# A list scheduler's assumed operand delay for TensorE, its price of a tile change and its priorities are replaced: encoder layer with RWKV-7 and differential attention, one core

## The chip, the cores and the metric

The kernel runs on one core of a Trainium2 chip. The time is device microseconds (us) of one execution. Engines are named as in the profile: PE (TensorE matmuls), PEld (TensorE weight loads), DVE (VectorE), ACT (ScalarE), POOL (GpSimd), SP (the queue that issues every DMA).

## The reference, cut to what matters

One encoder layer over two sequences (256 and 512 tokens, together T = 768, width 1024), in float32:

```
xn   = rmsnorm(x, norm_mix);  proj = xn @ w_in                  # 67 tiles of 128 columns
r, k, v, lw, la, lg = split(centred_shift(proj[:RWKV_COLS], mu)) # 27 of the tiles
y_a  = rwkv7_mixer(...)       # two scans (forward, backward) of 64x64 states, 16 heads
y_b  = diff_attention(...)    # 8 heads, partial rotary, two softmaxes each
merged = sigmoid(gate_a) * (y_a @ proj_a) + sigmoid(gate_b) * (y_b @ proj_b)
h    = x + merged @ w_out
out  = rmsnorm(h + square(relu(rmsnorm(h) @ w_mlp_in)) @ w_mlp_out, norm_final)
```

## The kernel before, in words

**The work.** Large products are split into three matmuls of a rounded type (fp32r: high by high, low by high, high by low), with 384 or 512 columns; the small ones of the scan and of attention are plain fp32. Operands of the large ones lie in region `x` (activations and weights), so the trace shows them as `bank<-x`. A weight comes by DMA in pieces of 128x256, one engine (ACT or DVE) rounds it to the high half, DVE subtracts to get the low half (`split`, called from `proj`), and only then TensorE can use it. PSUM has eight banks.

The scan is done in chunks of 64 tokens. There are 8 pairs of heads, and for each 4 jobs (two directions by two halves of the tokens), 32 in all. A job runs: `front` (decays, keys), group `g1` (matmuls 128x192), `solve` (a triangular inverse), `g2`, `duo` and `chain`. `solve` writes a matrix to DRAM, reads it back in another layout onto 96 partitions, runs 31 dependent steps on POOL (tile `f<-f`), writes the result to DRAM (`td`, four DMAs) and reads it back (four DMAs into `T_` and four into `tb`). Then DVE transposes 32x32 blocks (line 677), TensorE does a first half (six matmuls of 64x32 outputs), ACT or DVE copies the result, and TensorE does the second half (twelve matmuls 32x32). `duo` does groups of 128x128 matmuls, and `chain` carries the state from chunk to chunk: two matmuls with 64 columns, a copy from PSUM, two matmuls, and so on; each link needs the copy of the one before.

The projections that the scan doesn't need ("extra", 40 tiles of 48 matmuls) may stand anywhere and fill the time between. After the scans come attention (mixed with the last extras and `proja`), `projb`, `wout`, and the MLP.

**What sets the order.** `layer` first records some 18,500 operations with their dependencies in a `Plan`; `Plan.schedule` then simulates the five engines and emits, engine by engine, in the order that it chose. Every instruction is in-order on its engine, so this order is the kernel. At each step the scheduler takes the engine that is free first and, of the operations that are ready there, the one with the smallest key. The key is the place in the program (pair and job) plus `SHIFT` of the stage's name; `BIAS` decides, for work that more than one engine can do, which takes it; `LATE` says how many of the late pieces (`rest`) are recorded ahead of each attention head. When something is ready is worked out so, with `end` the simulated end of the operation it needs:

```
for s in o.next:
    s.wait -= 1
    for f in s.forms:
        s.ready[f] = max(s.ready[f], clk[e] if e == f == "pe" else end + AFTER[f])
```

and the choice on TensorE adds a price where the array's tile (128x128, 64x128, 128x64, 32x32) changes:

```
switch = lambda o: SWITCH * (e == "pe" and o.forms[e][2][0] != clock.tile)
for k, n, r, o in sorted((o.key + TURN * turns(o, e) + switch(o), o.n, r, o) for r, o in avail[e] if r <= t + 1e-3):
```

The simulated times and keys exist only while the program is built; on the chip nothing waits for them.

## Time and profile before

| | |
|---|---|
| median of 3 runs | 1998.9 us (1997.29 to 1999.33) |
| the profiled execution | 1998.35 us |
| its span, first to last instruction | 1996.5 us |
| PE busy | 1938.1 us (97%) |
| DVE busy | 1259.4 us (63%) |
| ACT busy | 871.9 us (44%) |
| POOL busy | 828.5 us (41%) |
| mean granted TensorE clock | 0.989 |

The page's share of busy time says which engine to look at; where that one stands still, and at which clock it runs, is read by stretches of the span. Stretches (us from the start): 0 to 28 norm of the input, 28 to 1050 projections and scans, 1050 to 1300 attention, 1300 to 1450 `projb` and `wout`, from 1450 the MLP. A matmul's end is modelled in the trace, so a busy PE is not a PE at its peak; an idle one surely waited.

### The profile page before, as it was taken

To read this page: it belongs to the slowest core of one execution; us is meant where nothing else is said; L and a number is where in the kernel's file an instruction comes from. 1 tells how busy PE (TensorE), PEld (TensorE's weight loads), DVE (VectorE), ACT (ScalarE), POOL (GpSimd) and SP (SyncE) were. 2 spreads that over 40 slices of the span, in tenths; PEclk is the share of its full clock that TensorE was granted. 3 is DMA by queue.
4 is the path that set the end of the run, shared out by engine and by line. 5 is a ranking of instruction groups with operands and counts; after the bars stand their busy time and mean duration, and the time that the engine had idled before them with its cause. 6 is when DMAs were issued, how large, how long until landed. Compare 5 with 4: busy or idle time off the path is not lost.

```text
span 1996.5 us, 36368 instructions
## 1 busy us (share of the span) xinstructions
PE 1938.1 (97%) x12698; PEld 1729.2 (87%) x12698; DVE 1259.4 (63%) x2750; ACT 871.9 (44%) x2178; POOL 828.5 (41%) x2177
## 2 busy tenths in 40 slices
PE   6999989999999999999999999999999999999998
PEld 6988879888888989889888776899899899989997
DVE  6977575666767677577534878574475555555545
ACT  5635465555656556565444778442221111111113
POOL 3278778786877878888770011011100000000000
PEclk9999999999999999999999999999999999999999
DMA  4133332222323232232343342254121111111111
GB/s 152 55 110 97 86 84 75 76 70 73 92 66 98 76 79 80 81 88 59 93 121 107 107 143 76 81 174 139 45 85 64 63 64 64 64 64 64 64 48 64
DMA packets 209787, 169.09 MB, mean 85 GB/s; under 512 B 106817, under 2 KB 176194, under 8 KB 209602
## 3 DMA queue, kind: packets, MB, share of 16 engines
q1 hardware_dynamic: 209602, 166.76, 28.1%
q8 instruction: 100, 1.64, 0.4%
q14 instruction: 85, 0.70, 0.1%
HBM read 137.97 MB, written 28.70 MB: 83 GB/s over the span
## 4 chain that ended last, share of the span: by engine, by line
PE 80%; DVE 11%; DMA 3%; ACT 2%; SPq 2%; issue 2%; POOL 0%; DVEq 0%; ACTq 0%; POOLq 0%
PE bank L693 78%; DVE g L622 3%; PE bank L698 2%; DVE x L622 2%; SPq L618 2%; DVE f L627 1%; DVE f L632 1%; DMA g<-dram 1%; DVE f L622 1%; DMA g<-in_w_in_dram 1%; DVE g L632 0%; DVE f L1012 0%; ACT f L669 0%; ACT x L638 0%; DVE g L677 0%
## 5 line engine op out<-in xcount | busy, mean ns | idle before, releaser
L693 PE MATMUL bank<-x 128*128 128x384 f32 (+1 forms) x5296 | 1146.9, 362 | 13.0 <-DVE x L622 4.6
L693 PEld LDWEIGHTS bank<-x 128*128 128x128 f32 x5296 | 929.6, 189 | 113.3 <-issue 18.9
L622 POOL TENSOR_TENSOR f<-f 96x60 f32<-96x60 f32 (+25 forms) x2081 | 758.9, 367 | 241.1 <-ACT f L638 41.5
L622 DVE TENSOR_TENSOR x<-g,x 128x256 fp32r<-128x256 f32 (+3 forms) x490 | 252.6, 522 | 159.7 <-ACT x L638 149.8
L693 PE MATMUL bank<-f,g 128*128 128x384 f32 x1920 | 338.2, 337 | 1.6 <-ACT f L669 1.6
L693 PEld LDWEIGHTS bank<-f,g 128*128 128x128 f32 x1920 | 336.1, 187 | 2.6 <-ACT f L669 1.9
L638 ACT ACTIVATE x<-g 128x256 fp32r<-128x256 f32 (+2 forms) x336 | 149.8, 453 | 351.6 <-PE bank L693 282.0
L622 DVE TENSOR_TENSOR g<-bank,g 128x128 f32<-128x128 f32 (+4 forms) x380 | 178.0, 479 | 179.2 <-PE bank L693 143.2
L638 ACT ACTIVATE g<-bank 64x128 f32<-64x128 f32 (+6 forms) x659 | 203.8, 324 | 189.3 <-PE bank L693 152.8
L622 POOL TENSOR_TENSOR g<-g 128x512 f32<-128x512 f32 (+1 forms) x9 | 15.4, 1711 | 592.3 <-DVE g L622 580.8
L693 PE MATMUL bank<-g,f 128*128 128x64 f32 (+3 forms) x1568 | 245.1, 293 | 4.5 <-DVE g L622 2.1
L693 PEld LDWEIGHTS bank<-g,f 128*128 128x128 f32 x1568 | 218.1, 191 | 27.0 <-DVE f L622 3.8
L622 DVE TENSOR_TENSOR g<-g 128x384 f32<-128x384 f32 (+6 forms) x234 | 116.7, 502 | 86.2 <-ACT g L669 73.8
L669 ACT ACTIVATE g<-bank 128x384 f32<-128x384 f32 x96 | 46.3, 491 | 246.5 <-PE bank L693 246.1
L638 ACT ACTIVATE f<-bank 128x192 f32<-128x192 f32 (+6 forms) x268 | 95.4, 387 | 109.9 <-PE bank L693 95.8
L693 PEld LDWEIGHTS bank<-g,g 64*128 64x128 f32 (+1 forms) x1728 | 119.7, 193 | 22.5 <-ACT g L638 10.7
L693 PE MATMUL bank<-g,g 64*128 64x128 f32 (+1 forms) x1728 | 136.5, 287 | 1.4 <-ACT g L638 1.4
L639 DVE CAST x<-g 128x384 fp32r<-128x384 f32 (+2 forms) x156 | 56.6, 364 | 54.7 <-PE bank L693 40.4
L698 PE MATMUL bank<-h,g 128*128 128x128 f32 x392 | 67.9, 294 | 19.0 <-DVE g L647 14.3
L693 PE MATMUL bank<-f 128*128 128x256 f32 (+2 forms) x352 | 86.0, 483 | 0.0
L693 PEld LDWEIGHTS bank<-g 32*32 32x32 f32 (+2 forms) x1378 | 54.8, 130 | 34.8 <-DVE g L677 14.4
L693 PE MATMUL bank<-g 32*32 32x32 f32 (+3 forms) x1378 | 73.9, 225 | 10.5 <-DVE g L677 9.0
(80 smaller groups left out, 1356.8 us busy)
## 6 DMA issues: line engine op xcount, KB each, us to landing
g<-in_w_in_dram SPq DMA_DIRECT2D x268, 128.0 KB
g<-in_w_dram SPq DMA_DIRECT2D x128, 256.0 KB
f<-dram SPq DMA_DIRECT2D x112, 192.0 KB
dram<-g SPq DMA_DIRECT2D x80, 192.0 KB
g<-in_x_dram SPq DMA_DIRECT2D x12, 512.0 KB
g<-dram SPq DMA_DIRECT2D x32, 192.0 KB
f<-dram SPq DMA_DIRECT2D x32, 144.0 KB
g<-in_pb_dram SPq DMA_DIRECT2D x16, 256.0 KB
```

Of the source, the lines that this page charges most:

```text
L618: pl.op([("sp", us, lambda: nc.sync.dma_start(out=chip(out), in_=chip(in_)), None)], [in_], [out], n / 250e3, tail)
L622: form = lambda x: (NAME[x], cost(x, (a, b), out), lambda: x.tensor_tensor(out=chip(out), in0=chip(a), in1=chip(b), op=op), None)
L627: emit = lambda: V.tensor_scalar(out=chip(out), in0=chip(a), scalar1=chip(s1), scalar2=chip(s2), op0=o0, op1=o1)
L632: emit = lambda: V.scalar_tensor_tensor(out=chip(out), in0=chip(a), scalar=chip(s), in1=chip(b), op0=o0, op1=o1)
L638: S: ("act", cost(S, (a,), out), lambda: S.activation(out=chip(out), in_=chip(a), func=AF.Copy, scale=1.0), None),
L639: V: ("dve", cost(V, (a,), out), lambda: V.tensor_copy(out=chip(out), in_=chip(a)), None),
L669: S.activation(out=chip(out), in_=chip(a), func=fn, scale=chip(scale), **k)
L693: emit = lambda: TE.matmul(chip(out), lhsT=chip(lhsT), rhs=chip(rhs), start=start, stop=stop)
L698: pl.op([("pe", 0.112, lambda: TE.transpose(chip(out), chip(a), chip(ident)), ((P, P), True, 0))], [a, ident], [out], tail=0.165)
```

## The change

Five tables of numbers are changed, and no line of the computation:

```
-AFTER = dict(pe=0.053, act=0.034, dve=0.033, pool=0.077, sp=0.026)
+AFTER = dict(pe=0.453, act=0.034, dve=0.033, pool=0.077, sp=0.026)
-SWITCH = 1.24
+SWITCH = 2.44
-LATE = (4, 4, 4, 3, 3, 4, 4, 2)
+LATE = (4, 4, 4, 3, 5, 4, 4, 2)
-SHIFT = {'proja': 3.64, 'rotate': -7.5, 'vs': -19.94, 'attn': -2.04, 'solve': -1.61, 'attend': -3.24, 'kkn': -4.92, 'proj': 4.76, 'g1': 1.9, 'g2': -1.95, 'chain': 1.9, 'norm': -6.88, 'x': -4.47, 'const': -7.99, 'lora': -10.39, 'front': 0.93, 'duo': -2.19, 'finish': -0.48, 'extra': 0.92, 'head': 3.89, 'projb': -6.52, 'wout': 18.65, 'mlp': -1.8}
-BIAS = {'x': {'dve': -0.25, 'act': 0.68, 'pool': -0.82}, 'a': {'dve': 2.31, 'pool': 5.49, 'act': -0.17}, 'b': {'dve': 0.49, 'pool': 4.32, 'act': -0.19}, 'c': {'act': -0.05, 'pool': 1.31, 'dve': 0.09}}
+SHIFT = {'proja': 3.68, 'rotate': -5.61, 'vs': -20.91, 'attn': -7.05, 'solve': -2.9, 'attend': -2.08, 'kkn': -4.32, 'proj': 4.7, 'g1': 1.71, 'g2': -1.95, 'chain': 1.9, 'norm': -6.7, 'x': -4.47, 'const': -8.17, 'lora': -9.73, 'front': 0.93, 'duo': -2.05, 'finish': -2.34, 'extra': 0.37, 'head': 2.79, 'projb': -6.57, 'wout': 17.42, 'mlp': -0.98}
+BIAS = {'x': {'dve': -0.67, 'act': 0.68, 'pool': -1}, 'a': {'dve': 2.31, 'pool': 5.25, 'act': 0.35}, 'b': {'dve': 0.49, 'pool': 4.03, 'act': -0.19}, 'c': {'act': 0.57, 'pool': 1.4, 'dve': 0.09}}
```

The scheduler now takes what another engine makes for TensorE as usable 0.4 us later than before, a tile change as twice as dear, and the stages' priorities are new numbers. The same operations are emitted: 10,177 matmuls and 1,373 DMAs in both; 45 fewer on ACT (2,010 to 1,965 activations), 31 more casts (237 to 268) and 15 more copies (91 to 106) on DVE, 19 more two-input operations on POOL (2,125 to 2,144). The order differs almost everywhere. Three places:

TensorE, the two halves of the 19th of the 32 solves; `64x32` is the first half, `32x32` the second, `bank<-x` are large matmuls of projections that don't depend on it. Before:

```order
L693 MATMUL bank_80<-x_88 128x384 x3
L693 MATMUL bank_76<-g_105 64x32 x6
L693 MATMUL bank_77<-x_88 128x384 x2
L693 MATMUL bank_79<-g_91 32x32 x2
L693 MATMUL bank_81<-g_91 32x32 x2
L693 MATMUL bank_79<-g_91 32x32 x2
L693 MATMUL bank_81<-g_91 32x32 x2
```

Now:

```order
L693 MATMUL bank_78<-x_88 128x384 x3
L693 MATMUL bank_80<-g_105 64x32 x6
L693 MATMUL bank_82<-x_88 128x384 x3
L693 MATMUL bank_78<-x_88 128x384
L693 MATMUL bank_75<-g_91 32x32 x2
L693 MATMUL bank_76<-g_91 32x32 x2
L693 MATMUL bank_75<-g_91 32x32 x2
L693 MATMUL bank_76<-g_91 32x32 x2
```

Four independent matmuls stand between the halves where there were two. Over the 32 solves the median goes from 2 to 4.

TensorE, links of the chain in the same job; `128x64` are the links (`g` the state's matrices, `f` what the copy has just written). Before:

```order
L693 MATMUL bank_78<-g_91,f_97 128x64 x2
L693 MATMUL bank_76<-x_88 128x384 x3
L693 MATMUL bank_78<-g_91,f_97 128x64 x2
L693 MATMUL bank_79<-x_88 128x384 x3
L693 MATMUL bank_78<-g_91,f_97 128x64 x2
```

Now:

```order
L693 MATMUL bank_78<-g_91,f_97 128x64 x2
L693 MATMUL bank_75<-x_88 128x384 x2
L693 MATMUL bank_80<-x_88 128x384 x3
L693 MATMUL bank_75<-x_88 128x384
L693 MATMUL bank_78<-g_91,f_97 128x64 x2
L693 MATMUL bank_75<-x_88 128x384 x2
```

Six stand between links where there were three; over all links that follow each other in one bank the commonest number goes from 3 (75 of 156) to 6 (82 of 161).

The SP queue, around the 18th solve; `dram<-f` 192x1x32 are its four result writes, `32x6x32` and `32x3x32` from the same `dram` its read-back, `128x768` the store of a finished pair, `dram<-g` 32x6x32 the input of a later solve. Before:

```order
L618 DMA dram_1934<-f_97 192x1x32
L618 DMA f_97<-in_glora_dram 128x128
L618 DMA g_91<-in_w_in_dram 128x256
L618 DMA dram_7156<-g_91 128x768
L618 DMA dram_1934<-f_97 192x1x32 x3
L618 DMA dram_882<-g_91 32x6x32
L618 DMA g_91<-dram_1934 32x6x32
L618 DMA g_91<-dram_1934 32x3x32
```

Now:

```order
L618 DMA dram_1875<-f_97 192x1x32 x4
L618 DMA f_97<-in_glora_dram 128x128
L618 DMA dram_7161<-g_91 128x768
L618 DMA g_91<-dram_1875 32x6x32
L618 DMA g_91<-dram_1875 32x3x32
```

The four writes stand together, and the later solve's input is behind the read-back. Over the 32 solves, DMAs of other work between a solve's first write and its last read-back go from 161 to 113, and those of them that are stores from 88 to 43.

## Rows read from the trace of the kernel before

**Rows 1.** The page's busy time of each engine.

```profile
PE 1938.1 (97%) x12698; PEld 1729.2 (87%) x12698; DVE 1259.4 (63%) x2750; ACT 871.9 (44%) x2178; POOL 828.5 (41%) x2177
```

**Rows 2.** Busy time by stretch, instructions in brackets; then TensorE clock, DMA share, GB/s.

```profile
core 0: us, PE busy (x) PEld busy (x) DVE busy (x) ACT busy (x) POOL busy (x), PEclk, DMA share, GB/s
0.00:28.00 28.00, 11.01 (x50) 9.38 (x51) 20.56 (x30) 19.84 (x43) 15.11 (x23) 0.88 0.56 189
28.00:100.00 72.00, 71.18 (x418) 69.11 (x417) 59.42 (x132) 41.21 (x93) 18.41 (x33) 1.00 0.23 70
100.00:600.00 500.00, 478.14 (x3740) 429.99 (x3738) 332.33 (x806) 265.13 (x704) 385.77 (x1069) 0.98 0.30 83
600.00:950.00 350.00, 347.12 (x2813) 314.31 (x2806) 246.75 (x564) 207.56 (x544) 285.32 (x782) 1.00 0.29 80
950.00:1050.00 100.00, 95.24 (x788) 86.51 (x788) 46.00 (x107) 48.22 (x134) 76.28 (x235) 0.97 0.39 110
1050.00:1450.00 400.00, 397.89 (x2173) 329.06 (x2171) 260.08 (x581) 210.57 (x499) 43.59 (x34) 1.00 0.35 108
1450.00:1985.00 535.00, 534.34 (x2720) 488.55 (x2721) 288.37 (x522) 74.56 (x151) 4.00 (x3) 1.00 0.19 62
1985.00:1997.00 12.00, 3.18 (x15) 2.29 (x13) 5.88 (x13) 4.82 (x13) 0.01 (x1) 0.74 0.42 160
```

**Rows 3.** Waits of PE's matmuls: for whom, us in total, times, longest.

```profile
PE bank L698 <- DVE g L647: 14.3, 4, 9.7
PE bank L693 <- DVE g L677: 9.0, 7, 2.9
PE bank L693 <- DVE x L622: 4.6, 10, 0.7
PE bank L693 <- ACT x L638: 4.3, 4, 3.1
PE bank L698 <- ACT g L648: 3.0, 1, 3.0
PE bank L693 <- DVE g L622: 2.4, 3, 1.9
PE bank L693 <- ACT f L669: 2.1, 2, 1.6
PE bank L693 <- DVE x L639: 1.5, 3, 1.1
PE bank L693 <- ACT g L638: 1.4, 2, 0.8
...
PE bank L693 <- DVE g L632: 0.2, 1, 0.2
```

**Rows 4.** Timeline, 443 to 449 us: start, length, engine, line, operation.

```profile
442.94 2.84 SPq L618 DMA_DIRECT2D g<-dram  x6
447.23 0.77 DVE L677 STREAM_TRANSPOSE g<-g 32x192 f32<-32x192 f32 x2 [3.93 <-DMA g<-dram]
448.06 0.85 PE L693 MATMUL bank<-g 128*64 128x32 f32 x12 [2.89 <-DVE g L677]
```

**Rows 5.** Timeline, 1012 to 1022 us.

```profile
1014.88 3.88 SPq L618 DMA_DIRECT2D g<-dram  x6
1017.88 0.42 ACT L638 ACTIVATE x<-g 128x256 fp32r<-128x256 f32 x1 [4.67 <-DMA g<-in_w_in_dram]
1018.35 3.18 PE L693 MATMUL bank<-x 128*128 128x384 f32 x9 [3.11 <-ACT x L638]
```

**Rows 6.** Timeline of PE, 560 to 575 us.

```profile
559.79 0.52 PE L693 MATMUL bank<-x 128*128 128x384 f32 x2
560.16 0.52 PE L698 MATMUL bank<-h,g 128*128 128x128 f32 x3
560.43 8.94 PE L693 MATMUL bank<-x 128*128 128x384 f32 x50
```

**Rows 7.** POOL's instructions on tile f: ns least, median, most; first and last start.

```profile
L622 POOL TENSOR_TENSOR f<-f x2081: 197/312/1587, 36.3 to 1049.4; 96x60 f32<-96x60 f32 x20, 128x256 f32<-128x256 f32 x11, 96x28 f32<-96x28 f32 x10, 96x66 f32<-96x66 f32 x10
```

**Rows 8.** Casts on DVE, by form: busy us, mean ns, idle before.

```profile
L639 DVE CAST x<-g 128x384 fp32r<-128x384 f32 x69 | 24.9, 361 | 2.4
```

## The prediction

> **What bounds the kernel now.** I read the page's busy times first, then busy time by stretch, the waits of PE, and the timeline around the two longest waits in the middle. TensorE is busy 97% of the span and the next engine 63% [rows 1], so the time is PE's work plus what PE loses. The stretches show where it loses [rows 2]. In the first 28 us it idles 17.0 us while the input is loaded and normalised, and in the last 12 us it idles 8.8: neither contains scan work, and I book nothing there. In between it is idle 0.8 + 21.9 + 2.9 + 4.8 + 2.1 + 0.7 = 33.2 us (length of each stretch less PE's busy time), nearly all of it from 100 to 600 and 950 to 1050 us. In these two the granted clock is also lower: 0.98 of 500 us and 0.97 of 100 us, so 10 + 3 = 13 us of full-speed time lost to the lower of the clock's two levels, 1.2 GHz. From 1050 us on the clock is at 2.4 GHz (1.00) and idle time is 2.8 us until the tail. So a different order of the same matmuls can win at most about 33 + 13 = 46 us, and only where scans and projections are mixed.
>
> The waits say what PE stood for [rows 3]. Transposes and copies for the start (line 698, 14.3 and 3.0 us) are in the first stretch. The others are three kinds. (a) The transposed read-back of a solve (line 677): 9.0 us in 7 waits, up to 2.9. (b) Rounded weights (tile `x`): 4.6 + 4.3 + 1.5 = 10.4 us in 17 waits, up to 3.1. (c) Results of ACT and DVE that go back to PE, the other groups: 2.4 + 2.1 + 1.4 and seven smaller ones of 1.3 down to 0.2, together 10.9 us, each under 2 us. Kinds (a) and (b) are DMAs that came late. At 448 us six read-back DMAs were issued in 2.84 us, DVE waited 3.93 us for them, and PE 2.89 us for DVE [rows 4]; at 1018 us a weight's DMA stood with six read-backs of 3.88 us in the SP queue, ACT waited 4.67 us for it and PE 3.11 us [rows 5].
>
> **The change part by part.** No operation is added or removed on PE or SP. What is moved, counted from the order: two more large matmuls between the halves of a solve, three more between the links of a chain. One such matmul takes 8.94 / 50 = 0.179 us [rows 6], so the cover grows by 0.36 and 0.54 us. Between a solve's first write and its last read-back stand 113 other DMAs instead of 161, and 43 stores instead of 88; a store waits in the queue for the engine that makes its data, and holds the read-back behind it.
>
> *(c), results of ACT and DVE.* At 10.9 us in some 20 waits their mean is about 0.55 us, as much as the added cover. Bounds: 0 (the longer ones are of late engines) and 10.9. I take -6, a little over half, since a few are 1.6 to 1.9 us long [rows 3] and would keep over 1 us.
>
> *(a), read-back.* Bounds 0 and 9.0. PE's use of the transposed blocks planned 0.4 us later takes 7 x 0.4 = 2.8 us by itself; the shorter queue takes more: a DMA of this queue costs 2.84 / 6 = 0.47 us of issue [rows 4], and (161 - 113) / 32 = 1.5 fewer stand in each solve's way, 0.7 us. Together about 1.1 us of a mean wait of 1.3 us. The longest keep a part, so I take -5.
>
> *(b), weights.* Bounds 0 and 10.4. Only the last hop is moved 0.4 us earlier; the 3.1 us wait would keep most of its length if the same DMAs met, 16 waits share the other 7.3 us and are no longer than about 1.1. I take -4.
>
> *The clock.* Bounds 0 and 13. The lower level follows the waits in these stretches (0.98 and 0.97 there, 1.00 in the stretch between with 2.9 us of idle in 350) [rows 2]. With 15 of some 30 us of waits gone I take the same half: -6.
>
> *The tile price.* Over PE's whole order the tile changes go from 378 to 372, the changes between fp32r and fp32 matmuls from 1,011 to 1,059. Around such a piece two large matmuls start within 0.37 us (0.185 each against 0.179), and the three small ones within 0.27 [rows 6]: no price above 0.1 us is visible. 48 x 0 to 0.1 gives 0 to +5; I take +1, near the row's value.
>
> *Work moved from ACT to DVE and POOL.* DVE's 46 more casts and copies cost 46 x 0.36 [rows 8] = 17 us of an engine that is idle 737 us of the span [rows 1]; PE's queue is the cover. If it fails at the place where a cast is waited for, one cast late is 0.36 us. I take +1 for that, and +2 for waits that the new order opens in attention and `wout`, where 2.1 us of idle [rows 2] leaves nothing to win; bounds 0 and +8, eight waits of a size like those in (c). The tail and the start: 0, their operations keep their places within a few rows.
>
> Sum: -6 - 5 - 4 - 6 + 1 + 1 + 2 = -17 us against the profiled execution's 1998.35 us (span 1996.5 and 1.85 around it), so 1981.4 us. The median of the runs lies 0.55 us higher; I forecast **1982 us**. With all bounds at their best the sum is -43 us (1956), at their worst +14 (2013).
>
> **A rule weighed against the trace.** POOL's instructions on tile `f`, of 96x28 to 128x256 elements, last from 197 to 1587 ns with a median of 312 [rows 7]; size explains a part of that spread, and the row doesn't tell whether some were held up. The Trainium skill (SBUF — State Buffer, "SBUF: two separate sides") says that VectorE and GpSimd share one pair of ports as an exclusive lock, held for a whole instruction by a VectorE operation in a two-port mode, and that the other blocks fully. That speaks against the move of casts to DVE, if they run in such a mode. No row here shows which mode they run in or who held POOL, so the trace neither bears the rule out nor excludes it. By the row alone the move costs nothing beyond the +1 above; by the rule it would cost what the third rival says.
>
> **The rivals.**
>
> *No change.* The waits of (a) and (b) come from DMAs that are 3 to 5 us late [rows 4, 5]; cover of 0.4 to 0.5 us doesn't reach them, and others of the same size open where the queue now meets. What speaks for it: from 600 to 950 us, with the same tight order, PE is idle only 2.9 us in 350 and the clock is full [rows 2], so tight links by themselves cost almost nothing. Against it: the shorter queue around read-backs. Then only (c) gives some 3 us, and the tile and cast prices take 2 back: 1998 us.
>
> *Slower, by a stretched chain.* Six links and one solve of a job get 6 x 0.54 + 0.36 = 3.6 us longer, 32 jobs 115 us. It is hidden as long as PE has independent matmuls and POOL sets the pace: it is busy 285 of 350 us from 600 to 950 [rows 2], its last scan step starts at 1049 us [rows 7]. It decides where the independent projections run out before the last pair is through; then the last pair's four jobs, 14 us, are exposed, and with the other gains at half (-7) the time is 1998.9 + 7 = 2006 us. Against it: in the order the last extras stand further behind than before, not earlier, and POOL has 65 us free in that stretch.
>
> *DVE holds POOL.* 46 operations of 0.36 us [rows 8], if each holds one POOL step and the scans wait for POOL, add 17 us, which eats the gain: 1999 us. The mechanism is the Trainium skill's rule of the shared port (SBUF — State Buffer, "SBUF: two separate sides"). Against it: POOL's free 65 us, and some of the 46 lie in the MLP, where it has nothing to do (4.0 us busy) [rows 2].
>
> *The change does not do what it says* (later use is only in the plan): the order's counts exclude this for chains and solves; what is left of it is the first rival.
>
> **How the numbers follow.** Forecast (some half of the waits and of the clock loss go): 0.72. No change 0.11. Stretched chain 0.10. DVE holds POOL 0.07. The measurement tells no less than 0.2%, 4 us, from no change. The forecast's own spread runs from 1960 to 1996; about 0.02 of it lies above 1994.9. Faster: 0.70, the forecast without that. Within 4 us of 1998.9: 0.09 of the first rival, 0.05 of the third (DVE holds POOL) and the 0.02 of the forecast: 0.16. Slower: the 0.10 of the second, with 0.02 of the first and 0.02 of the third that end above: 0.14. The range, 1964 to 2003 us, reaches from three quarters of the full gain (0.75 x 46 = 35 us) to the middle of the rivals; I leave out some 0.08 below and 0.11 above.
>
> **What would show it.** Right: waits for line 677 and tile `x` sum to under 11 us where they were 19.4, the other groups to under 6, the clock from 100 to 600 us at 0.99 or more, PE idle there under 12 us. The three rivals show as: the same sums with other addresses (no change); PE idle and POOL idle together from 950 to 1100 us (chain); a median of POOL's steps above 312 ns and PE waiting for line 677 in more than 7 solves (port). The prediction is wrong if PE's idle time between 28 and 1450 us falls as said and the time doesn't, or if the start or the tail moves by more than 3 us.

## The result, and the profile after

The changed kernel takes **1964.74 us** (median of 4 runs, 1963.67 to 1964.96) against 1998.1 us for the kernel before beside it (4 runs, 1995.6 to 1999.33): a ratio of 0.983, 95% interval 0.9814 to 0.9845, a gain of 33.4 us. The forecast was 1982 us: the direction and the range held, the gain is twice the one forecast.

The profiled execution took 1964.61 us, its span is 1962.8 us. Busy time of each engine, to be laid beside [rows 1]:

```profile
PE 1916.3 (98%) x12698; PEld 1731.5 (88%) x12698; DVE 1275.6 (65%) x2776; ACT 847.4 (43%) x2133; POOL 851.3 (43%) x2196
```

PE runs the same number of instructions and is busy 21.8 us less, so most of the gain is not idle time. The span is 33.7 us shorter; it splits into three parts that need the page alone. **Idle**, the span less PE's busy time, falls from 58.4 to 46.5 us: -11.9. **Clock loss**, the span times what the mean granted clock lacks of 1, falls from 0.011 x 1996.5 = 22.0 to 0.005 x 1962.8 = 9.8 us: -12.2 (the clock's rounding makes that uncertain by some 1 us; the trace after has no clock entry before 28.9 us, so up to 0.12 x 28 = 3.4 us of this part, from the first row of [rows 2], may belong to the next one). The rest, PE's busy time less the clock loss, is the **full-speed work**. It would not change with the order if the same matmuls cost the same wherever they stand, and yet it falls from 1916.1 to 1906.5 us, -9.6; with the start's 3.4 us counted here it is -13.0, and the clock's part -8.8.

By stretch, the same view as [rows 2] (the 1.00 of the first row stands for no entry):

```profile
core 0: us, PE busy (x) PEld busy (x) DVE busy (x) ACT busy (x) POOL busy (x), PEclk, DMA share, GB/s
0.00:28.00 28.00, 11.75 (x51) 10.55 (x52) 19.75 (x33) 18.87 (x41) 14.29 (x23) 1.00 0.57 189
28.00:100.00 72.00, 71.55 (x420) 70.11 (x418) 58.98 (x131) 42.67 (x97) 19.17 (x32) 1.00 0.23 70
100.00:600.00 500.00, 484.09 (x3903) 446.51 (x3903) 349.91 (x841) 276.66 (x740) 407.48 (x1127) 0.99 0.32 87
600.00:950.00 350.00, 346.68 (x2851) 320.93 (x2849) 247.88 (x571) 198.38 (x523) 287.13 (x785) 1.00 0.30 81
950.00:1050.00 100.00, 99.43 (x858) 92.78 (x857) 44.66 (x107) 47.13 (x130) 59.83 (x180) 1.00 0.46 131
1050.00:1450.00 400.00, 397.61 (x2080) 331.00 (x2078) 282.40 (x607) 200.78 (x475) 60.73 (x48) 1.00 0.34 104
1450.00:1950.00 500.00, 500.00 (x2526) 455.69 (x2525) 264.55 (x478) 56.86 (x115) 1.29 (x1) 1.00 0.19 60
1950.00:1962.80 12.80, 5.19 (x23) 3.95 (x22) 7.50 (x15) 6.07 (x16) 1.41 (x1) 0.79 0.43 164
```

From 28 to 1450 us PE is idle 0.5 + 15.9 + 3.3 + 0.6 + 2.4 = 22.7 us where it was 0.8 + 21.9 + 2.9 + 4.8 + 2.1 = 32.5; the clock is at 0.99 and 1.00 in the two stretches where it was 0.98 and 0.97. From 600 to 950 us idle time is no better (3.3 against 2.9 us), and yet 38 more matmul records fit into that stretch (2851 against 2813). That hints at the third part and doesn't measure it, since 24 of the 38 are 32x32 matmuls, which are short.

A fixed stretch holds other work in the two kernels. To compare like with like, here is the stretch from the first 32x32 matmul of the first solve to the start of the last scan step on POOL, and the one from there to the first `f,g` 128x384 matmul (behind attention); first the kernel before, then the change:

```profile
143.70:1049.40 905.70, 879.52 (x7101) 791.85 (x7100) 594.09 (x1398) 506.37 (x1344) 714.44 (x1994) 0.98 0.30 83
1049.40:1318.50 269.10, 267.12 (x1501) 209.37 (x1501) 185.43 (x461) 171.00 (x422) 26.38 (x24) 1.00 0.34 102
```

```profile
142.20:1023.00 880.80, 866.94 (x7163) 800.47 (x7163) 606.48 (x1423) 500.76 (x1333) 719.35 (x1995) 1.00 0.32 87
1023.00:1286.80 263.80, 261.41 (x1461) 204.46 (x1460) 185.34 (x448) 167.49 (x417) 34.76 (x32) 1.00 0.33 99
```

The scans take 24.9 us less and do 62 more matmuls; attention takes 5.3 less, having 40 fewer. The two together make 30.2 of the 33.7 us. In the scans idle time falls from 26.2 to 13.9 us and the clock is up from 0.98.

PE's waits, the view of [rows 3]:

```profile
PE bank L698 <- DVE g L647: 11.7, 2, 9.8
PE bank L693 <- DVE x L622: 5.4, 8, 3.5
PE bank L693 <- ACT x L638: 4.6, 7, 2.0
PE bank L693 <- ACT g L638: 3.3, 4, 2.3
PE bank L698 <- ACT g L648: 3.0, 1, 3.0
PE bank L693 <- DVE g L622: 1.7, 5, 0.5
PE bank L693 <- ACT f L669: 1.6, 1, 1.6
PE bank L698 <- POOL g L649: 1.5, 1, 1.5
PE bank L693 <- DVE g L639: 1.3, 1, 1.3
PE bank L693 <- DVE x L639: 1.1, 2, 0.6
...
PE bank L693 <- DMA g<-dram: 0.2, 1, 0.2
```

The wait for line 677 (the transposed read-back of a solve), 9.0 us before, is gone. Weights (tile `x`) cost 11.1 us where they cost 10.4. All other groups but those of the input's norm (lines 647 and 648) sum to 11.5 where they were 10.9.

**Where the full-speed work went.** A matmul's end is modelled, so a small delay of the next one needn't show as idle time. Three rows of PE's matmuls by form (busy us, mean ns of one, then the idle time before), before:

```profile
L693 PE MATMUL bank<-g,f 128*128 128x64 f32 x768 | 115.6, 271 | 0.5 <-DVE f L622 0.2
L693 PE MATMUL bank<-g,f 128*128 128x192 f32 x384 | 72.5, 334 | 3.6 <-DVE g L622 1.9 <-DVE f L632 1.3 <-ACT f L669 0.5
L693 PE MATMUL bank<-g,f 128*128 128x128 f32 x384 | 51.8, 280 | 0.3 <-DVE g L622 0.2
```

and after:

```profile
L693 PE MATMUL bank<-g,f 128*128 128x64 f32 x768 | 109.3, 261 | 2.9 <-ACT g L638 2.6 <-DVE f L622 0.3
L693 PE MATMUL bank<-g,f 128*128 128x192 f32 x384 | 71.3, 328 | 0.8 <-DVE g L622 0.5 <-ACT g L638 0.2
L693 PE MATMUL bank<-g,f 128*128 128x128 f32 x384 | 51.6, 279 | 0.2 <-DVE g L622 0.2
```

The chain's links, the first row, hold PE 6.3 us less for the same 768 matmuls, while the idle time charged to them was only 0.5 us before. The three rows together fall by 7.7 us; the rest of the 9.6 is not assigned to rows here. The timeline of PE shows it in single links (start, length, operation; the trace has two instructions for each matmul of a link, so a link is four). Before, around 704 us:

```profile
703.21 0.79 PE L693 MATMUL bank<-x 128*128 128x384 f32 x3
703.84 0.59 PE L693 MATMUL bank<-g,f 128*128 128x64 f32 x4
704.24 0.60 PE L693 MATMUL bank<-x 128*128 128x384 f32 x2
```

After, around 684 us:

```profile
683.07 1.32 PE L693 MATMUL bank<-x 128*128 128x384 f32 x6
684.23 0.56 PE L693 MATMUL bank<-g,f 128*128 128x64 f32 x4
684.59 0.60 PE L693 MATMUL bank<-x 128*128 128x384 f32 x2
```

Behind three large matmuls the four of a link hold the queue for 704.24 - 703.84 = 0.40 us; behind six, 684.59 - 684.23 = 0.36. In neither does the timeline put an idle time in brackets: the stop lies inside the modelled length of the matmuls. Over all links of four that a large matmul follows at once, the same distance has a median of 0.41 us before (132 links) and 0.36 in the change (126).

Where PE's rows hide the stop, those of the weight loads (PEld) show it. At the same two places, before:

```profile
703.21 0.47 PEld L693 LDWEIGHTS bank<-x 128*128 128x128 f32 x3
703.77 0.52 PEld L693 LDWEIGHTS bank<-g,f 128*128 128x128 f32 x4
```

and after:

```profile
683.07 1.00 PEld L693 LDWEIGHTS bank<-x 128*128 128x128 f32 x6
684.06 0.58 PEld L693 LDWEIGHTS bank<-g,f 128*128 128x128 f32 x4
```

Before, the link's first weight load starts 703.77 - 703.68 = 0.09 us after the last one ended; after, it starts at once. The row of the weight loads of all `g,f` matmuls (links and the two groups) has its idle time behind the second bar; before, then after:

```profile
L693 PEld LDWEIGHTS bank<-g,f 128*128 128x128 f32 x1568 | 218.1, 191 | 27.0 <-DVE f L622 3.8 <-ACT g L638 3.2 <-issue 2.5
L693 PEld LDWEIGHTS bank<-g,f 128*128 128x128 f32 x1568 | 226.6, 191 | 11.2 <-ACT g L638 3.4 <-DVE g L622 1.9 <-ACT f L638 0.8
```

It falls by 15.8 us, where the three matmul rows had 4.4 us of idle time before and 3.9 after.

### The profile page after: what moved, and what is told of

Read it like the earlier page. It is cut to its first block, busy times and chain, and to the rows that moved or that the text cites. A ratio compares the mean times of both kernels' runs of the same rounds, so it can differ in the third digit from the quotient of the medians.

```text
span 1962.8 us, 36390 instructions
## 1 busy us (share of the span) xinstructions
PE 1916.3 (98%) x12698; PEld 1731.5 (88%) x12698; DVE 1275.6 (65%) x2776; ACT 847.4 (43%) x2133; POOL 851.3 (43%) x2196
## 3 DMA queue, kind: packets, MB, share of 16 engines
q1 hardware_dynamic: 209602, 166.76, 28.9%
## 4 chain that ended last, share of the span: by engine, by line
PE 63%; DVE 4%; POOL 1%; ACT 1%; DMA 1%; issue 1%; SPq 0%; POOLq 0%; DVEq 0%; ACTq 0%
PE bank L693 61%; PE bank L698 2%; POOL f L622 1%; DVE g L622 1%; DVE x L622 1%; DVE f L632 0%; DVE f L622 0%; DVE f L627 0%; ACT g L669 0%; DVE g L1270 0%; ACT L1581 0%; DVE g L632 0%; DVE f L1012 0%; DMA g<-dram 0%; DMA g<-in_pa_dram 0%
## 5 line engine op out<-in xcount | busy, mean ns | idle before, releaser
L622 POOL TENSOR_TENSOR f<-f 96x60 f32<-96x60 f32 (+26 forms) x2081 | 763.0, 369 | 219.4 <-ACT f L638 34.5
L638 ACT ACTIVATE x<-g 128x256 fp32r<-128x256 f32 (+2 forms) x326 | 144.6, 448 | 341.5 <-PE bank L693 299.7
L638 ACT ACTIVATE g<-bank 128x128 f32<-128x128 f32 (+6 forms) x648 | 199.0, 324 | 192.6 <-PE bank L693 150.6
L693 PE MATMUL bank<-g,f 128*128 128x64 f32 (+2 forms) x1568 | 236.0, 286 | 4.1 <-ACT g L638 2.9
L693 PEld LDWEIGHTS bank<-g,f 128*128 128x128 f32 x1568 | 226.6, 191 | 11.2 <-ACT g L638 3.4
L669 ACT ACTIVATE g<-bank 128x384 f32<-128x384 f32 x96 | 46.5, 492 | 243.0 <-PE bank L693 242.5
L638 ACT ACTIVATE f<-bank 128x192 f32<-128x192 f32 (+5 forms) x259 | 89.5, 377 | 114.0 <-PE bank L693 102.7
L693 PEld LDWEIGHTS bank<-g,g 64*128 64x128 f32 (+1 forms) x1728 | 116.5, 188 | 20.4 <-issue 11.1
L639 DVE CAST x<-g 128x512 fp32r<-128x512 f32 (+2 forms) x166 | 60.4, 365 | 56.0 <-PE bank L693 46.1
L622 POOL TENSOR_TENSOR x<-g,x 128x256 fp32r<-128x256 f32 x29 | 25.2, 869 | 148.7 <-ACT x L638 73.7
L669 ACT ACTIVATE g<-g 128x512 f32<-128x512 f32 (+4 forms) x90 | 49.4, 551 | 70.2 <-DVE g L622 60.7
```

What stands on the lines that cost most here:

```text
L622: form = lambda x: (NAME[x], cost(x, (a, b), out), lambda: x.tensor_tensor(out=chip(out), in0=chip(a), in1=chip(b), op=op), None)
L638: S: ("act", cost(S, (a,), out), lambda: S.activation(out=chip(out), in_=chip(a), func=AF.Copy, scale=1.0), None),
L639: V: ("dve", cost(V, (a,), out), lambda: V.tensor_copy(out=chip(out), in_=chip(a)), None),
L669: S.activation(out=chip(out), in_=chip(a), func=fn, scale=chip(scale), **k)
L693: emit = lambda: TE.matmul(chip(out), lhsT=chip(lhsT), rhs=chip(rhs), start=start, stop=stop)
```

## The experiments

**Theory**: the gain hangs on one number, the delay `AFTER["pe"]`. It puts more independent matmuls behind each operand, and saves read-back waits, the clock that they cost, and short stops inside PE's busy time; the priorities only have to suit it. **First rival**: the priorities or the tile price bring the gain by themselves, through the SP queue. **Second rival**: orders scatter so much that the change is merely a lucky one.

All runs in one table, so that each can be set beside the others. Each ratio is to runs of the kernel before on the same chip. Idle, clock loss and full-speed work are worked out from each page as above; "links" is the busy time of the 128x64 row; "L677" the wait of PE for read-backs.

| kernel | us | ratio (95%) | idle | clock loss | full-speed work | links | L677 |
|---|---|---|---|---|---|---|---|
| before | 1998.1 | | 58.4 | 22.0 | 1916.1 | 115.6 | 9.0 |
| the change | 1964.74 | 0.983 (0.9814 to 0.9845) | 46.5 | 9.8 | 1906.5 | 109.3 | 0 |
| e1, delay only | 1980.55 | 0.9904 (0.988 to 0.9928) | 59.8 | 11.9 | 1907.3 | 109.8 | 5.3 |
| e2, tile price only | 2005.5 | 1.003 (1.0017 to 1.0043) | 62.9 | 18.1 | 1924.8 | 115.0 | 12.0 |
| e3, priorities only | 2014.61 | 1.0076 (1.0051 to 1.01) | 66.5 | 22.1 | 1924.6 | 115.4 | 12.4 |
| e4, change without delay | 2000.93 | 1.0007 (0.9991 to 1.0022) | 59.5 | 12.0 | 1928.1 | 115.1 | 6.4 |
| f1, delay for the chain | 1993.74 | 0.9977 (0.9967 to 0.9988) | 57.5 | 14.0 | 1922.0 | 109.5 | 7.2 |
| f2, delay for all but it | 1983.45 | 0.9927 (0.9909 to 0.9945) | 56.4 | 13.9 | 1913.2 | 115.7 | 1.2 |
| g1, before moved, draw 1 | 2012.61 | 1.0081 (1.0066 to 1.0096) | 61.5 | 20.1 | 1931.9 | 116.0 | 6.3 |
| h1, change moved, draw 1 | 1979.19 | 0.9913 (0.9899 to 0.9928) | 57.2 | 11.9 | 1907.8 | 108.6 | 2.6 |
| g2, before moved, draw 2 | 2021.7 | 1.0117 (1.0091 to 1.0144) | 75.1 | 14.2 | 1932.3 | 115.0 | 9.6 |
| h2, change moved, draw 2 | 2001.17 | 1.0018 (1.0005 to 1.003) | 65.8 | 28.0 | 1905.6 | 108.7 | 4.5 |
| e6, change, delay 0.253 | 2000.44 | 1.0009 (0.9996 to 1.0022) | 68.9 | 22.0 | 1909.0 | 109.0 | 1.8 |
| k1, change, delay 0.653 | 1973.22 | 0.987 (0.9849 to 0.989) | 56.1 | 9.9 | 1906.7 | 110.4 | 2.2 |
| e7, change, delay 0.853 | 1968.34 | 0.9852 (0.9833 to 0.987) | 52.1 | 13.8 | 1900.6 | 108.1 | 2.0 |
| j1, change, small moves 1 | 1973.92 | 0.9872 (0.9854 to 0.9891) | 53.2 | 15.8 | 1903.6 | 109.2 | 0.9 |
| j2, change, small moves 2 | 1977.38 | 0.9893 (0.9876 to 0.9911) | 54.2 | 13.8 | 1906.8 | 109.2 | 2.3 |
| l1, change, old SHIFT | 1982.39 | 0.9918 (0.9902 to 0.9935) | 60.2 | 17.8 | 1903.0 | 110.2 | 2.9 |

The column of the clock has a weakness. As in the trace of the change, eleven of the eighteen traces have no clock entry in the first 25 us; in the other seven a lower level there counts for 1.7 to 5.1 us. Compare these two columns only to that. With the start left out of all clock losses, the full-speed work is 1900.6 to 1912.4 us in the ten kernels with a delay of 0.253 or more for all operands and 1919.5 to 1932.3 in the six with 0.053, so this comparison holds. The links' row doesn't follow the clock: e4 has a mean clock of 0.994 as e1, and 115.1 us against 109.8; h2 has the lowest, 0.986, and 108.7.

### The tables one by one (e1 to e4)

e1, on the kernel before:

```
-AFTER = dict(pe=0.053, act=0.034, dve=0.033, pool=0.077, sp=0.026)
+AFTER = dict(pe=0.453, act=0.034, dve=0.033, pool=0.077, sp=0.026)
```

> The kernel before with AFTER's pe alone at 0.453. By its order, the median number of matmuls between the halves of a solve is 4 (2 before), between chain links 6 (3 before), and 98 other DMAs stand in the solves' read-backs (161 before, 113 in the change). Delay theory (the 0.4 us is the whole gain): 1960 to 1970 us, no PE wait for line 677, mean clock 0.994 or more. Priority theory (the new SHIFT, BIAS and LATE are the gain): 1990 to 2005 us. Scatter theory (any new order is some 15 us away from another, whatever its numbers mean): anywhere from 1965 to 2010 us, not near the change.

1980.55 us. One number is worth 1 - 0.9904 = 1.0%, more than half of the gain. Idle time does not move at all (59.8 against 58.4 us): the gain is 10.1 us of clock (up to 3.4 of it at the start, on paper) and 8.8 us of full-speed work, and the row of the links does what it does in the change. The time lies above the 1960 to 1970 us that the delay theory gave for the whole gain, and waits for line 677 are left (5.3 us).

e2, on the kernel before:

```
-SWITCH = 1.24
+SWITCH = 2.44
```

> The kernel before with SWITCH alone at 2.44. Its counts of cover (2 and 3) and of other DMAs (159) are those of before. Delay theory: 1993 to 2003 us, no change; waits for line 677 stay at 5 to 12 us. Priority theory: the same. Scatter theory: 10 us or more away from before, to either side.

e3, on the kernel before, all priorities, with delay and tile price as before:

```
-LATE = (4, 4, 4, 3, 3, 4, 4, 2)
+LATE = (4, 4, 4, 3, 5, 4, 4, 2)
...
```

and behind it the lines of `SHIFT` and `BIAS` as in the diff of the change.

> The kernel before with SHIFT, BIAS and LATE of the change, AFTER and SWITCH as before. Cover 2 and 3, 157 other DMAs, as before. Delay theory: 1990 to 2003 us. Priority theory: 1962 to 1975 us. Scatter theory: 10 us or more from before, to either side, and the parts don't add up to the change.

The tile price alone makes the kernel 0.3% slower, the priorities alone 0.8%: both are slower than the delay theory's ranges (up to 2003 us), so these two kernels scatter by more than it allowed, and e3's 1962 to 1975 us of the priority theory is missed by 40. The first rival falls. The queue as the cause is weakened too: in e3 the stores between a solve's first write and last read-back went from 88 to 73, and the waits for line 677 rose from 9.0 to 12.4 us.

e4, on the change:

```
-AFTER = dict(pe=0.453, act=0.034, dve=0.033, pool=0.077, sp=0.026)
+AFTER = dict(pe=0.053, act=0.034, dve=0.033, pool=0.077, sp=0.026)
```

> The change with AFTER's pe alone put back to 0.053. Cover 2 and 3, 156 other DMAs, as before. Delay theory: the gain is gone, 1990 to 2003 us, with waits for line 677 and stretches of lower clock back. Priority theory: 1963 to 1975 us. Scatter theory: between, and not the sum of the parts.

2000.93 us, as the delay theory had it: priorities and tile price together bring nothing without the delay, and full-speed work (1928.1 us) is above that of the kernel before. The effects don't add: the delay is worth 18 us in the old order and 36 in the new one. The tile price has its part in that. e4 differs from e3 by it alone and is 2014.61 - 2000.93 = 13.7 us faster, though on the kernel before the same price cost 0.3%. So the new priorities cost 16 us without the delay at the old tile price and 2 us at the new one; with delay and new tile price both bring 1980.55 - 1964.74 = 16 us together. The change with the old tile price was not run, so how these 16 us divide between priorities and tile price is open but for l1, below.

### Which operands the delay serves (f1, f2)

On the kernel before, the delay for some of PE's operations only; f1 for those of the chain, f2 (with `!=`) for all others:

```
-                    s.ready[f] = max(s.ready[f], clk[e] if e == f == "pe" else end + AFTER[f])
+                    s.ready[f] = max(s.ready[f], clk[e] if e == f == "pe" else end + AFTER[f] + 0.4 * (f == "pe" and s.label[0] == "chain"))
```

> The kernel before, with the 0.4 us added only where TensorE's consumer is a link of the chain. By its order 6 matmuls between links (3 before), 2 between the halves of a solve (as before), 123 other DMAs in the read-backs (161 before). Three sums are read: idle = span less PE busy (before 58.4 us), clock loss = span times one less the mean granted clock (before 22.0), busy at full clock = the rest (before 1916.1; the change 1906.5; AFTER alone 1907.3). Hidden-link theory (a link whose copy is just in time loads its weights late, some 0.1 us, which the modelled end of the matmul before it covers, so that PE looks busy): busy at full clock falls to 1906 to 1910, all that AFTER alone gave; idle and clock loss within 10 us of before. Visible-wait theory (the busy time fell because other waits did): busy at full clock stays at 1914 to 1920. Time by the first 1985 to 1995 us, by the second 1995 to 2003.

> The kernel before, with the 0.4 us added for every consumer on TensorE but the chain's links. 3 matmuls between links (as before), 4 between the halves of a solve (2 before), 119 other DMAs. Hidden-link theory: busy at full clock stays at 1913 to 1919 us (1916.1 before), what is gained is idle time for line 677 and clock loss, 5 to 12 us together: 1986 to 1996 us. Visible-wait theory: busy at full clock falls to 1906 to 1910 and the time to 1978 to 1986.

f1 gains 0.23%, f2 0.73%, and together that is the 0.96% of e1; with a scatter between orders as in the next section, that the sum fits so well may be chance. f1's time is in the range of the hidden-link theory, but its full-speed work is in that of neither: 1922.0 us, above the kernel before, although the links' row did fall. f2 has the full-speed work of the hidden-link theory (1913.2 us) and, with 1983.45 us, the time of its rival. The rows by form say where the time went; f1:

```profile
L693 PE MATMUL bank<-g,f 128*128 128x64 f32 x768 | 109.5, 260 | 0.7 <-DVE f L622 0.7
L693 PE MATMUL bank<-g,f 128*128 128x192 f32 x384 | 78.1, 340 | 3.0 <-DVE g L622 1.9 <-ACT f L669 1.1
```

and f2:

```profile
L693 PE MATMUL bank<-g,f 128*128 128x64 f32 x768 | 115.7, 272 | 3.2 <-ACT g L638 1.8 <-DVE f L622 1.2
L693 PE MATMUL bank<-g,f 128*128 128x192 f32 x384 | 70.9, 328 | 1.9 <-DVE f L627 0.7 <-DVE g L622 0.7 <-ACT f L669 0.5
```

With the chain alone the links' row falls by 6.1 us and the row of the 128x192 group rises by 5.6; with all but the chain the links' row stays and the other one falls by 1.6. So cover taken for one kind of operand may have been missing at the next; what stood ahead of the 128x192 groups was not counted. The links themselves are clear: the median of the distance defined above is 0.36 us in f1, as in the change, and 0.41 in f2, as before, and the weight loads' row has 15.7 and 24.7 us of idle time:

```profile
L693 PEld LDWEIGHTS bank<-g,f 128*128 128x128 f32 x1568 | 224.1, 192 | 15.7 <-issue 2.7 <-ACT f L669 2.6 <-DVE f L622 1.7
L693 PEld LDWEIGHTS bank<-g,f 128*128 128x128 f32 x1568 | 220.4, 191 | 24.7 <-ACT g L638 2.9 <-DVE f L622 2.5 <-POOL f L622 1.7
```

That stops at the links are hidden in PE's busy time, and that cover ends them, is shown by this pair.

In f2 PE's wait for read-backs falls to 1.2 us in two waits, with 119 other DMAs between a solve's first write and its last read-back; in f1 it is 7.2 us with 123. Nearly the same queue, and only f2 has the longer cover of the solves (4 large matmuls between the halves against 2): that speaks for the cover as what ends these waits. It is not the whole of it, since e1, with 4 and with only 98 other DMAs, keeps 5.3 us in six waits.

### Is it the order, or luck (g1, h1, g2, h2)

The `SHIFT` numbers of both kernels, moved by the same random amounts (normal, 0.4), two draws; g1 and g2 on the kernel before, h1 and h2 on the change. h1's edit of the change:

```
-SHIFT = {'proja': 3.68, 'rotate': -5.61, 'vs': -20.91, 'attn': -7.05, 'solve': -2.9, 'attend': -2.08, 'kkn': -4.32, 'proj': 4.7, 'g1': 1.71, 'g2': -1.95, 'chain': 1.9, 'norm': -6.7, 'x': -4.47, 'const': -8.17, 'lora': -9.73, 'front': 0.93, 'duo': -2.05, 'finish': -2.34, 'extra': 0.37, 'head': 2.79, 'projb': -6.57, 'wout': 17.42, 'mlp': -0.98}
+SHIFT = {'proja': 4.2, 'rotate': -5.03, 'vs': -20.88, 'attn': -7.36, 'solve': -3.34, 'attend': -2.07, 'kkn': -4.73, 'proj': 4.13, 'g1': 1.79, 'g2': -1.9, 'chain': 2.12, 'norm': -7.07, 'x': -4.47, 'const': -8.2, 'lora': -10.33, 'front': 1.15, 'duo': -1.92, 'finish': -1.38, 'extra': 0.45, 'head': 2.73, 'projb': -6.08, 'wout': 17.5, 'mlp': -0.62}
```

> A measure of scatter: the kernel before with every number of SHIFT moved by a random amount (normal, 0.4; AFTER and all else as before). Cover 2 and 3 as before, 145 other DMAs. If the numbers of before are a finely tuned point, 2000 to 2020 us, with busy at full clock at 1914 to 1926; if any priorities do as well, 1990 to 2005 us. The size of the move tells what a difference of two orders is worth as evidence.

> The same random moves on the SHIFT of the change (AFTER's pe at 0.453). Cover 4 and 6 as in the change, 113 other DMAs. If the priorities chosen with random lateness lie on a flat piece, 1962 to 1972 us; if the last 16 us against AFTER alone (1980.6) are a lucky point, 1975 to 1995 us. By either, busy at full clock stays at 1904 to 1911, because the cover is still there.

> A second draw of the random moves on the SHIFT of the kernel before (AFTER's pe 0.053). The first gave 2012.6 us, 14 above before. Two-part theory (the delay is worth some 33 us at equal tuning; numbers tuned for the delay in force another 14): 2005 to 2020 us, and the link row (fp32 matmuls with 64 columns) stays at 115 to 117 us busy. Scatter theory: anywhere from 1985 to 2025.

> The second draw on the SHIFT of the change (AFTER's pe 0.453). The first gave 1979.2 us. Two-part theory: 1972 to 1987 us, some 33 below the draw of before; link row at 108 to 111 us; waits for line 677 under 6 us. Scatter theory: anywhere from 1960 to 2000.

At the same moves the change's tables are worth 33.4 us (2012.61 to 1979.19) and 20.5 us (2021.7 to 2001.17), where the unmoved pair gives 33.4. h1 landed where a lucky point was expected (1975 to 1995 us), not a flat piece. g1 lies in the range of a finely tuned point, with more full-speed work than expected (1931.9 us against up to 1926); g2 is 1.7 us above the two-part theory's range; h2 missed its 1972 to 1987 us by 14, and even the scatter theory's 2000 by 1. h2's full-speed work is low, as in the change (1905.6); it lost 28.0 us to the clock and 65.8 to idle time. Much of the clock's part lies near the start: h2 and then the change, from 28 to 149 us,

```profile
28.00:149.00 121.00, 111.27 (x607) 105.54 (x608) 84.94 (x193) 52.19 (x121) 52.62 (x127) 0.90 0.25 73
28.00:149.00 121.00, 114.61 (x701) 111.25 (x700) 92.15 (x217) 58.26 (x141) 58.95 (x144) 0.97 0.30 88
```

0.10 x 121 = 12 us, against 0.03 x 121 = 4 us in the change. So the second rival is half right: full-speed work follows the delay in every draw, and that part is not luck; idle time and clock scatter by the order, and moves of 0.4 cost the change 14 and 36 us.

### How long a delay (e6, e7, k1)

The change with `AFTER["pe"]` at 0.253, 0.853 and 0.653:

```
-AFTER = dict(pe=0.453, act=0.034, dve=0.033, pool=0.077, sp=0.026)
+AFTER = dict(pe=0.253, act=0.034, dve=0.033, pool=0.077, sp=0.026)
...
+AFTER = dict(pe=0.853, act=0.034, dve=0.033, pool=0.077, sp=0.026)
...
+AFTER = dict(pe=0.653, act=0.034, dve=0.033, pool=0.077, sp=0.026)
```

> The change with AFTER's pe at 0.253, half way. Cover by the order: 3 between the halves of a solve, 5 between links. Two-part theory: the numbers are tuned for another delay (as with AFTER alone, 1980.6, and the change without it, 2000.9), so the time lies between these, 1982 to 1996 us, and the link row at 109 to 113 us. If the priorities were robust by themselves, 1964 to 1975.

> The change with AFTER's pe at 0.853, twice the cover: 7 between the halves of a solve, 8 between links, 97 other DMAs. Two-part theory with a delay that saturates: nothing is left to cover at the links (row at 108 to 110 us), tuning is lost: 1970 to 1985 us. Stretched-chain theory (more cover lengthens the scans): 1985 to 2010 us, with PE and POOL idle together after 950 us.

> The changed kernel with the delay for TensorE at 0.653 in place of 0.453, all else as in the change. It stands between 0.453 (1964.7 us) and 0.853 (1968.3). If the time falls on smoothly with the cover and flattens, 1960 to 1970 us, waits for read-backs under 2.5 us and the link's row near 108; if each order scatters by itself, anything from 1965 to 1995, with the excess in PE's idle time and in the clock, not in the link's row.

In us: 2000.9 at 0.053 (e4), 2000.44, 1964.74, 1973.22 and 1968.34 at 0.853. Only a part of that is a curve. Full-speed work is: 1928.1, 1909.0, 1906.5, 1906.7, 1900.6, most of it won by 0.253 and the rest nearly flat. Idle time (59.5, 68.9, 46.5, 56.1, 52.1) and clock loss (12.0, 22.0, 9.8, 9.9, 13.8) don't follow the delay. All three missed their first theory's range: e6 1982 to 1996 us, k1 1960 to 1970, and e7, which came out faster, 1970 to 1985. k1's excess is where its rival put it, in idle time (the links' row is a little up as well, 110.4). With 0.853 some 8 large matmuls stand between two links where 6 do in the change, and the time is only 3.6 us longer: here chains could be stretched that far at little cost. None of the three beats the change.

### The last 16 us: how sharp, and which table (j1, j2, l1)

The change with `SHIFT` moved by small amounts (normal, 0.1), two draws, and with the `SHIFT` of the kernel before (l1); j1, then l1, against the change:

```
+SHIFT = {'proja': 3.56, 'rotate': -5.57, 'vs': -20.81, 'attn': -7.1, 'solve': -3.03, 'attend': -2.09, 'kkn': -4.27, 'proj': 4.81, 'g1': 1.59, 'g2': -2.08, 'chain': 1.97, 'norm': -6.65, 'x': -4.32, 'const': -8.07, 'lora': -9.74, 'front': 0.9, 'duo': -1.79, 'finish': -2.37, 'extra': 0.29, 'head': 2.68, 'projb': -6.56, 'wout': 17.43, 'mlp': -1.01}
...
+SHIFT = {'proja': 3.64, 'rotate': -7.5, 'vs': -19.94, 'attn': -2.04, 'solve': -1.61, 'attend': -3.24, 'kkn': -4.92, 'proj': 4.76, 'g1': 1.9, 'g2': -1.95, 'chain': 1.9, 'norm': -6.88, 'x': -4.47, 'const': -7.99, 'lora': -10.39, 'front': 0.93, 'duo': -2.19, 'finish': -0.48, 'extra': 0.92, 'head': 3.89, 'projb': -6.52, 'wout': 18.65, 'mlp': -1.8}
```

> The changed kernel with its SHIFT numbers moved by small random amounts (normal, 0.1, first draw); delay, bias, lateness and switch as in the change. Theory: the delay carries most of the gain and the chosen priorities are one good order among many, found with lateness in the simulation and so not sharp; small moves then give 1962 to 1978 us, with the row of the 128x64 link at 108 to 110 us of busy time. Rival: the priorities are one lucky order, and any move loses all that they add to the delay; then 1979 to 2002 us, as with the large moves, the link's row unchanged at 108 to 110.

> As the first small draw, with a second one. Theory: 1962 to 1978 us. Rival of the lucky order: 1979 to 2002 us. Both draws together under 1978 speak for the first, both over for the second; one of each leaves it open.

> The changed kernel with the SHIFT numbers of before; BIAS, LATE, SWITCH and the delay as in the change. If the new SHIFT numbers carry what the priorities add to the delay, 1977 to 1990 us, near the delay alone in the old order (1980.6); if BIAS, LATE and SWITCH carry it, 1962 to 1974. The link's row at 108 to 110 us either way.

1973.92 and 1977.38 us: both inside the range of a broad optimum, but at its upper end. A quarter of the large moves costs 9 and 13 of the 16 us, so "broad" is too much said. l1 gives 1982.39 us, near e1's 1980.55: without the new `SHIFT` numbers, `BIAS`, `LATE` and the tile price add nothing to the delay. Whether `SHIFT` brings the 16 us without them was not run, and by e3 and e4 the tile price matters beside it. What is lost in l1 is 13.7 us of idle time and 8.0 of clock, with 3.5 us less full-speed work. By stretch, l1:

```profile
600.00:950.00 350.00, 343.96 (x2829) 318.59 (x2827) 238.75 (x545) 203.21 (x531) 277.75 (x761) 1.00 0.30 83
...
1050.00:1450.00 400.00, 389.60 (x2061) 321.98 (x2060) 269.48 (x589) 198.97 (x481) 54.42 (x42) 0.99 0.33 103
```

Behind the scans PE is idle 10.4 us where it was 2.4 in the change. Waits of PE from 1050 to 1450 us in l1:

```profile
PE bank L693 <- ACT g L638: 6.5, 1, 6.5
PE bank L693 <- DVE g L622: 1.5, 1, 1.5
PE bank L693 <- POOL g L622: 1.1, 1, 1.1
```

One wait of 6.5 us is most of it. In l1, then, the idle time is a few long waits at a place where the change has none. Why the change's order has the least idle time of all 18 kernels, stage by stage, these runs don't settle, nor whether another set of numbers would do better still.

## Why the prediction was right and wrong

**The bound** was read rightly: PE, and only where scans and projections are mixed; 30.2 of the 33.7 us came from the scans and the attention behind them. The ceiling of 46 us, though, counted only idle time and clock. (The worst sum is off by one: the bounds +5 and +8 give +13, 2012 us, not +14.)

**The step that failed** is the sentence in the first rival that "tight links by themselves cost almost nothing", and with it the sum, which had no term for full-speed work. It was read from 2.9 us of idle time in 350 [rows 2]. PE's idle time can't show it. Full-speed work fell by 9.6 us (13.0 with the start counted here), which is more than half of the some 17 us that the forecast lacked; 6.3 of it stand in the links' row, and the weight loads' row shows the stops that went. In the runs it is tied to the delay: 1900.6 to 1909.0 us in the ten kernels with 0.253 or more for all operands, 1916.1 to 1932.3 in the six with 0.053, 1913.2 and 1922.0 in the two halves. The links' row is 108.1 to 110.4 us in every kernel with more cover for the chain and 115.0 to 116.0 in every one without.

**The clock**: -6 booked, -12.2 measured, -8.8 without the start, where up to 3.4 may be on paper. The mechanism held and the size was short: by the rows of the stretches the 13 us of the middle became 0.01 x 500 = 5. From 100 to 600 us half came back as said (0.99), in the last 100 us of the scans all (1.00 for 0.97), with 4 us less idle time. Clock and idle time don't fall in proportion: e1 won 6.7 to 10.1 us of clock with as much idle time as before.

**The waits.** Cover, tile price and casts were booked at -6 - 5 - 4 + 4 = -11 us, and idle time from 28 to 1450 us fell by 9.8. The sum was right by luck, by errors that cancel. (a) Read-backs: -5 booked, -9.0 measured; the cover of 0.36 us and the shorter queue were weighed as two parts, and f2, with 1.2 us left, speaks for the cover. (b) Weights: -4 booked, +0.7 measured. That late DMAs are behind them doesn't hold for the longest one after, 3.5 us at 106 us: PE waited for the split on DVE, and DVE's timeline shows no idle time ahead of it from 100 us on; DVE was busy with work of the scan. Whether the casts moved to DVE made it late is not shown. (c) Other results of ACT and DVE: -6 booked, +0.6 measured (1.5 us after is line 649, in the norm of the start); some short ones went (three groups of DVE's tile `f` were 2.5 us in 5 waits and one of 0.6 is left), and new ones of 2.3 and 1.3 us came. So the marks set out for the waits were missed: 11.1 us against "under 11" for line 677 and `x`, 11.5 against "under 6" for the others, 15.9 us of idle time from 100 to 600 against "under 12". The booked cost of +4 is not seen by itself: from 1050 to 1450 us idle time is 2.4 us against 2.1, and a price of tile or type changes would stand in full-speed work, which fell.

**What no term stood for**: that the tables work together. Delay and priorities give -18 and +16 us alone; that the forecast of -17 is what the delay alone brought is chance. Priorities found with one delay and one tile price lose without them (e3, e4) and gain with them.

**The rivals.** *No change* falls: the time moved by 33 us. Its argument, that tight links cost almost nothing, is the step that failed. *Stretched chain* falls: from 950 to 1050 us PE idles 0.6 us, and with 8 matmuls between links (e7) the kernel is still 1.5% faster than before. *DVE holds POOL* falls: steps of POOL on tile `f` after,

```profile
L622 POOL TENSOR_TENSOR f<-f x2081: 199/312/1829, 36.5 to 1023.0; 96x60 f32<-96x60 f32 x19, 96x48 f32<-96x48 f32 x12, 96x28 f32<-96x28 f32 x11, 96x66 f32<-96x66 f32 x11
```

have the same median of 312 ns as in [rows 7] with 46 more casts and copies on DVE, and no solve keeps PE waiting for line 677. A median can't tell of 46 steps in 2081; the row's busy time can, and it rises by 4.1 us (758.9 to 763.0), a quarter of the rival's 17. The Trainium skill (SBUF — State Buffer, "SBUF: two separate sides") says that a VectorE operation in a two-port mode, once it has the shared ports, locks GpSimd out for its length. If these casts do so, it costs POOL's steps here no more than that.

**The start and the tail** moved by 1.5 us (first solve, 143.7 to 142.2) and by 0.7 (from PE's last matmul to the end of the span, 8.4 to 7.6), under the 3 us allowed.

## What to carry to other kernels

On an in-order engine that is 97% busy, an assumed delay for operands from other engines is a cheap lever: here one number gave 1%, by placing more independent matmuls behind each hop (0.23% for the chain's operands, 0.73% for all others). Don't take "idle" for all that an engine loses: compare the busy time of one form, with the same count, between orders, since short stops hide inside modelled lengths, and read the idle time of the weight loads beside that of the matmuls. And choose priorities together with the delay and the tile price: taken out of the change, the delay costs 36 us and the new `SHIFT` numbers 18, of 33 that all bring. At moves of 0.1 in its priorities this list schedule lost 0.5 and 0.6%, at 0.4 from 0.7 to 1.9%, so a verdict on one setting needs several draws.

## What the runs showed of the hardware

A late operand holds TensorE without an idle entry in the rows of its matmuls: 0.40 us for a link's four against 0.36, and 6.3 us over the 768 of a kernel. It shows as idle time ahead of the weight loads, 27.0 us before and 11.2 after. The granted clock is lower where waits are, but not in proportion to them: 26.2 us of idle time in the scans went with 0.98, 13.9 with 1.00, and from 28 to 149 us 9.7 us of idle time went with 0.90 in h2, 6.4 with 0.97 in the change.
